# A hybrid layer on one core: two key projections and a gate block change places in the state space stage

## The chip, the cores and the metric

The kernel runs on one core of a Trainium2 chip. The metric is the device time of one execution in microseconds, the median of several; lower is better. All times of instructions come from one profiled execution.

The core has TensorE (PE: matmuls, and transposes made as matmuls), VectorE (DVE), ScalarE (ACT), GpSimd (POOL) and SyncE (SP), which issues the DMAs here. Each engine works through its own instructions in order and waits on semaphores for the others. Matmul results go to PSUM, in banks of 128 x 512 fp32.

## What is computed

One layer for 512 tokens of width 1024: a normed input is projected; a state space mixer (S5) and an attention with compressed, selected and windowed keys (NSA) work on parts of the projection; gates merge them; a feed-forward part with a convolution and a last gated part follow. The pieces that matter here:

```python
z = n1 @ w_in[i]
y_ssm = s5_mixer(z[..., OFF_SSM:OFF_Q], ...)
y_nsa = nsa_mixer(z[..., OFF_Q:OFF_KV], z[..., OFF_KV:OFF_NSA_GATE], ...)
merge = jax.nn.sigmoid(z[..., OFF_MERGE:].astype(jnp.float32))
mixed = merge[..., :D_MODEL] * (y_ssm @ w_br_ssm[i]) + merge[..., D_MODEL:] * (y_nsa @ w_br_nsa[i])

# s5_mixer: a linear recurrence over time, 32 groups of 64 complex states
_, states = lax.associative_scan(combine, (a_seq, bu), axis=1)
y = einsum(c_re, real(states)) - einsum(c_im, imag(states))
# nsa_mixer: keys of blocks of 32 tokens are made by a small network
kc = compress_blocks(k_cmp, pe_k, wk1, wk2)
vc = compress_blocks(v_cmp, pe_v, wv1, wv2)
```

All of it is in fp32. A product of two fp32 matrices is made of three matmuls of rounded parts: high x high, low x high, high x low.

## The kernel before

**Projections.** `proj` (L202 and on, with `mm3` at L81 to L84) multiplies one 128-column block of `w_in` with the normed input: 8 x 3 = 24 matmuls of 512 columns into a PSUM bank of the tag `acc`, of which there are two. The weights are brought by a DMA on SyncE's queue into one of three buffers `wr`; ScalarE copies their high part `wh` (L75), and GpSimd or VectorE subtracts it to get the low part `wl` (L54). There are two buffers each of `wh` and `wl`, so the weights of one projection can only be split when the projection two places before it has let go of them. In this stage GpSimd makes `wl`.

**The state space stage** works in four quarters. `ssm_quarter` is a generator in two halves. The first half prepares a quarter: products `z` (VectorE) and `x` (GpSimd) of the recurrence's coefficients, spread by ScalarE into `Z` and `CX`, transposed on TensorE (`wbps`, L798), copied by ScalarE (`WB`), and multiplied with the inputs (`wps`, L807). The second half makes its outputs: VectorE rotates (`f`, `wps`), runs four scans (L852) with small carries `c` between, and rotates back into the states `sr`; TensorE makes a small matrix `tps` (L832), which ScalarE copies as `tz`; then TensorE multiplies `sr` and `tz` into `yps` (L870, L872), VectorE adds a skip term (`un`) and ScalarE takes the gelu (`yT`).

**What else runs there**: `compress_in(i)`, a projection whose result ScalarE and VectorE copy, two copies each, into `FL`; `keys(br)`, a projection whose result goes to `KK`, the high part by ScalarE and the low part by VectorE, half by half (a half's subtraction by VectorE needs ScalarE's copy of that half); `compress(i)`, 32 small matmuls `hps` (L917), a transposing copy `hT`, a gelu `hid` on ScalarE and a last product `kps` (L932 or L942); and `gate_done(i)`, a projection with a tanh into `t1`. Behind the stage follow the softmaxes of `compressed`, with the gates 1 to 3 between them, a gated unit `glu`, and attention, whose matmuls are mixed with more gate projections.

**What sets the order.** The code is recorded by a scheduler, which orders each engine's instructions itself: mainly by the order in which the code hands them over, by when it expects their inputs, and by edges written with `issue_after`, which hold instructions back behind a named one. It also hands out the PSUM banks of a tag. A call that stands earlier in the code thus goes ahead of what follows it where both could go.

Of the kernel before, what the change touches and what calls it, by code (L numbers as in the profile page):

```python
# [44 lines left out]
def hybrid_kernel(ctx: ExitStack, tc: tile.TileContext, A, out):  # L45
# [7 lines left out]
    def tt(o, a, b, op, e=V):  # L53
        e.tensor_tensor(o, a, b, op=op)  # L54
# [19 lines left out]
    def copy(o, a):  # L74
        S.activation(o, a, AF.Copy)  # L75
# [27 lines left out]
    def slot(p, tag, shape, dt, name):  # L103
        return p.tile(shape, dt, tag=tag, name=name, bufs=1)
# [97 lines left out]
    def proj(c0, e=V, w=None):  # L202
        hi, lo = w or wload("w_in", INW, 0, c0, KD, P, e)
        ps = bank("acc", "pj")
        for k in range(KD):
            mm3(ps, hi[:, k], lo[:, k], n1h[:, k], n1l[:, k], k == 0, k == KD - 1)
        return ps
# [686 lines left out]
    def compress_in(i):  # L894
        ps = proj(OFF_KV + i * P, G)
        for g in range(2):
            for j in range(2):
                x = ps[64 * g:64 * g + 64, j:j + 1]
                (V.tensor_copy if g else copy)(
                    FL[64 * j:64 * j + 64, i, :, g, 0:NCMP - 1],  # L900
                    bass.AP(tensor=x.tensor, offset=x.offset, ap=[x.ap[0], [2, 16], [16, NCMP - 1]]))

    def keys(br):
        ps = proj(OFF_KV + 256 + 256 * br, G)
        for g in range(2):
            s0, o0 = 64 * g, 64 * (1 - g)
            copy(KK[s0:s0 + 64, br, g], ps[s0:s0 + 64])
            tt(KK[o0:o0 + 64, br, g], ps[s0:s0 + 64], KK[s0:s0 + 64, br, g], SUB)
# [44 lines left out]
    def t1(dt_):  # L953
        return t1s[dt_ // 4][:, dt_ % 4]

    def gate(dst, w):
        ps = bank("acc", "pj")
        for k in range(KD):
            mm3(ps, w[0][:, k], w[1][:, k], n1h[:, k], n1l[:, k], k == 0, k == KD - 1)
            yield  # L960
        S.activation(dst, ps, AF.Tanh, scale=0.5)

    def gate_weights(i, e=G):
        return wload("w_in", INW, 0, OFF_M + i * P, KD, P, e)

    def gate_done(i):
        for _ in gate(t1(i), gate_weights(i)):
            pass
# [3 lines left out]
    for q in range(4):  # L972
        if q < 3:
            next(quarters[q + 1])
        next(quarters[q])
        if q == 0:
            compress_in(0)
            compress_in(1)
        elif q == 1:
            compress(0)  # L980
            keys(0)
            t1s.append(slot(py, "t8", [P, 4, T], F32, "t1a"))
        elif q == 2:
            VC = compress(1)
            keys(1)
            gate_done(0)
    sM.close()
    sS.close()
    PTC = slot(pa, "ptc", [P, 2, 2, T], F32R, "PTC")

    def compressed(qt):
        qs_ = slice(qt * P, (qt + 1) * P)
        ps = bank("s", "cs")
        for i in range(4):
            PE.matmul(ps[:, P * i:P * i + P], QT[:, i, 0, qs_], KC[:, :, i // 2], start=True, stop=False)
            PE.matmul(ps[:, P * i:P * i + 64], QT[:, i, 1, qs_], KC[:, 0, i // 2], start=False, stop=True)
        sc = pw.tile([P, H, NCMP], F32, name="cmps", tag="mg")
        shc = [P, H, NCMP]
        sums = ps.rearrange("p (i x h n) -> p x i h n", i=4, x=2, h=2)
        sc4 = sc.rearrange("p (i h) n -> p i h n", i=4)  # L1000
        tt(sc4, sums[:, 0], maskc[:, qt, None, None, :].to_broadcast([P, 4, 2, NCMP]), ADD)
        tt(sc4, sc4, sums[:, 1], ADD)
        mx, su = small("cmx", H, 2), small("csu", H, 2)
        V.tensor_reduce(mx, sc, AX.X, ALU.max)
        tt(sc, sc, mx[:, :, None].to_broadcast(shc), SUB)
        with tc.issue_after(ys_at) if qt >= 2 else nullcontext():
            S.activation(sc, sc, AF.Exp, scale=HD ** -0.5)
        V.tensor_reduce(su, sc, AX.X, ADD)
        V.reciprocal(su, su)
        tt(su, su, gates[:, qt, 0:8], MUL)  # L1010
        if qt == 0:
            ts(su, su, rowok)
        tt(sc, sc, su[:, :, None].to_broadcast(shc), MUL)
        return sc

    def compressed_t(qt, sc):
        pc = bank("t", "pct")
        for g in range(2):
            PE.transpose(pc[:, g * P:(g + 1) * P], sc[:, 4 * g:4 * g + 4].rearrange("p h n -> p (h n)"), ident)
        qs_ = slice(qt * P, (qt + 1) * P)  # L1020
        split(PTC[:, 0, :, qs_], PTC[:, 1, :, qs_], pc[:, 0:256].rearrange("p (g t) -> p g t", g=2))
# [11 lines left out]

    scs = {}
    for dt_ in range(4):
        if dt_:
            gate_done(dt_)
        scs[dt_] = compressed(dt_)
        if dt_:
            compressed_t(dt_ - 1, scs[dt_ - 1])  # L1040
# [697 lines left out]
    with tc.manual_schedule(engines={mybir.EngineType.PE, mybir.EngineType.SP}):  # L1738
# [328 lines left out]
        keys = {"22": 0, "s1": 1, "s2": 2, "s3": 3, "s4": 0}  # L2067
# [192 lines left out]
```

## Time and profile before

| | us |
|---|---|
| median of 3 runs | 785.84 (785.81 to 785.86) |
| the profiled execution | 786.37 |
| its span, from the first to the last instruction | 784.6 |
| VectorE busy | 611.0 |
| ScalarE busy | 437.0 |
| GpSimd busy | 233.3 |

The span is a little shorter than the execution that it was taken from. Busy times add up what an engine did. A timeline row gives an instruction's start, its duration, the engine, the line, output and inputs, shapes and a count of merged instructions, and in square brackets how long the engine had been idle before it and who released it. Matmuls overlap, so the time that one really costs is the distance between two starts and not the duration in its row. A matmul of fp32 operands that are not split shows as two in the trace and as one in the order of the program.

### The profile page before, as it was taken

What the parts mean: (1) busy time and instruction counts of PE and PEld (TensorE: products, weight loads), DVE (VectorE), ACT (ScalarE), POOL (GpSimd) and SP (SyncE); (2) the same over time, 40 slices, a digit from 0 to 9 for tenths busy, and PEclk for the clock granted to TensorE, in tenths of its full rate; (3) what the DMA queues carried; (4) which work ended last, traced back from release to release, by engine and by line L of the source; (5) the groups of instructions that cost most, each with busy time, mean ns of one, the idle gap of its engine ahead of it and who ended that gap; (6) DMA issues with size and microseconds to landing.
All of it is one profiled execution on the core that took longest, in us unless ns stands there. A gap on an engine that the chain in (4) does not pass through costs nothing.

```text
span 784.6 us, 12279 instructions
## 1 busy us (share of the span) xinstructions
PE 767.0 (98%) x4362; PEld 646.7 (82%) x4362; DVE 611.0 (78%) x1192; ACT 437.0 (56%) x779; POOL 233.3 (30%) x263
## 2 busy tenths in 40 slices
PE   9999999999999999999999999999999999999993
PEld 7887778888888888888998888888888888888883
DVE  7987999776677739799757887988977586877586
ACT  6835645656676745444644554455444555645654
POOL 3577533126464625001032122221222110000125
PEclk9999999999999999999999999999999999999997
DMA  9954131423234327310266887778887366578752
GB/s 343 372 160 150 54 96 42 126 78 114 75 93 124 108 72 277 103 33 27 82 215 219 286 296 263 262 255 294 318 266 267 115 252 213 206 231 289 271 215 107
DMA packets 52077, 144.54 MB, mean 184 GB/s; under 512 B 6192, under 2 KB 8624, under 8 KB 52016
## 3 DMA queue, kind: packets, MB, share of 16 engines
q1 hardware_dynamic: 51440, 142.71, 53.1%
q10 hardware_dynamic: 576, 1.05, 0.4%
q8 instruction: 34, 0.56, 0.3%
q14 instruction: 27, 0.22, 0.1%
HBM read 112.28 MB, written 27.26 MB: 178 GB/s over the span
## 4 chain that ended last, share of the span: by engine, by line
PE 87%; DVE 6%; DMA 2%; issue 2%; ACT 1%; POOL 1%; SPq 0%; POOLq 0%; DVEq 0%; ACTq 0%
PE pj L82 6%; PE pj L83 6%; PE pj L84 6%; PE ua L1664 5%; PE ua L1665 5%; PE ub L1664 5%; PE ub L1670 5%; PE ua L1670 5%; PE ub L1665 5%; PE p L84 4%; PE p L82 4%; PE p L83 4%; PE sps L1089 2%; PE ptp L1109 2%; PE br L82 2%; PE br L84 2%
## 5 line engine op out<-in xcount | busy, mean ns | idle before, releaser
L54 POOL TENSOR_TENSOR wl<-wr,wh 128x1024 fp32r<-128x1024 f32 x45 | 114.4, 2543 | 315.0 <-ACT wh L75 185.7
L75 ACT ACTIVATE wh<-wr 128x1024 fp32r<-128x1024 f32 x96 | 100.7, 1050 | 59.8 <-issue 19.8
L82 PE MATMUL pj<-n1h,wh 128*128 128x512 f32 x224 | 90.9, 406 | 0.5 <-DVE QT L54 0.5
L83 PE MATMUL pj<-n1l,wh 128*128 128x512 f32 x224 | 87.9, 392 | 0.0
L84 PE MATMUL pj<-n1h,wl 128*128 128x512 f32 x224 | 87.8, 393 | 0.0
L54 DVE TENSOR_TENSOR wl<-wr,wh 128x1024 fp32r<-128x1024 f32 (+1 forms) x51 | 62.0, 1216 | 18.6 <-ACT wh L75 18.6
L1664 PE MATMUL ua<-n2h,wh 128*128 128x512 f32 x160 | 62.4, 390 | 0.0
L1665 PE MATMUL ua<-n2l,wh 128*128 128x512 f32 x160 | 62.3, 389 | 0.0
L1664 PE MATMUL ub<-n2h,wh 128*128 128x512 f32 x160 | 62.3, 389 | 0.0
L1665 PE MATMUL ub<-n2l,wh 128*128 128x512 f32 x160 | 62.2, 389 | 0.0
L63 DVE SCALAR_TENSOR_TENSOR cv<-ua,cols,cv 128x511 f32<-128x511 f32 (+1 forms) x44 | 32.9, 749 | 23.5 <-ACT cv L1511 22.7
L84 PEld LDWEIGHTS pj<-n1h,wl 128*128 128x128 f32 x224 | 42.1, 188 | 8.8
L82 PEld LDWEIGHTS pj<-n1h,wh 128*128 128x128 f32 x224 | 42.1, 188 | 8.3 <-DVE QT L54 0.9
L83 PEld LDWEIGHTS pj<-n1l,wh 128*128 128x128 f32 x224 | 42.2, 188 | 7.4 <-issue 0.2
L63 DVE SCALAR_TENSOR_TENSOR cv<-ub,cols,cv 128x511 f32<-128x511 f32 (+1 forms) x44 | 32.9, 748 | 15.8 <-ACT cv L1511 14.8
L60 POOL TENSOR_SCALAR pr<-pr,su,gates 128x512 f32<-128x512 f32 (+2 forms) x64 | 38.6, 619 | 16.6 <-DVE su L1101 16.3
L75 ACT ACTIVATE ph<-ptp 128x128 fp32r<-128x128 f32 (+1 forms) x64 | 27.8, 435 | 26.2 <-PE ptp L1109 26.0
L54 DVE TENSOR_TENSOR pl<-ptp,ph 128x128 fp32r<-128x128 f32 (+1 forms) x64 | 31.0, 486 | 14.3 <-ACT ph L75 13.3
L1670 PE MATMUL ub<-n2h,wl 128*128 128x512 f32 x160 | 39.5, 389 | 0.0
L1670 PE MATMUL ua<-n2h,wl 128*128 128x512 f32 x160 | 39.5, 389 | 0.0
L75 ACT ACTIVATE ffa<-cv 128x256 fp32r<-128x256 f32 x22 | 9.2, 418 | 53.0 <-DVE cv L54 46.5
L1100 ACT ACTIVATE pr<-pr,nb 128x512 f32<-128x512 f32 (+2 forms) x64 | 35.5, 558 | 3.0 <-DVE nb L1098 2.9
(522 smaller groups left out, 2091.7 us busy)
## 6 DMA issues: line engine op xcount, KB each, us to landing
wr<-in_w_up_dram SPq DMA_DIRECT2D x44, 512.0 KB, 4.4
wr<-in_w_in_dram SPq DMA_DIRECT2D x28, 512.0 KB, 3.8
b<-in_w_down_dram SPq DMA_DIRECT2D x22, 512.0 KB, 6.0
bs<-b SPq DMA_DIRECT2D x44, 256.0 KB, 5.5
ue<-bs SPq DMA_DIRECT2D x21, 512.0 KB, 4.8
wr<-in_w_down_dram SPq DMA_DIRECT2D x11, 512.0 KB, 5.3
gs<-gph SPq DMA_DIRECT2D x10, 512.0 KB, 6.1
gs<-gpl SPq DMA_DIRECT2D x10, 512.0 KB, 6.8
```

Of the source, the lines that this page charges most:

```text
L54: e.tensor_tensor(o, a, b, op=op)
L60: e.tensor_scalar(o, a, s1, s2, op0=op0, op1=op1)
L63: e.scalar_tensor_tensor(o, a, s, b, op0=op0, op1=op1)
L75: S.activation(o, a, AF.Copy)
L82: PE.matmul(ps, lh, rh, start=start, stop=False, skip_group_check=goes_on)
L83: PE.matmul(ps, lh, rl, start=False, stop=False, skip_group_check=goes_on)
L84: PE.matmul(ps, ll, rh, start=False, stop=stop, skip_group_check=goes_on)
L1089: PE.matmul(o, self.QQ[:, x, qt * P:(qt + 1) * P], KK[:, :, self.g, :w] if both else KK[:, self.br, self.g, :w], start=x == 0, stop=x == 1)
L1100: S.activation(pp, pp, AF.Exp, bias=nb, scale=-1.0, accum_out=su)
L1664: PE.matmul(ps, hi[:, k], n2h[:, k], start=k == 0, stop=False)
L1665: PE.matmul(ps, hi[:, k], n2l[:, k], start=False, stop=False)
L1670: PE.matmul(ps, lo[:, k], n2h[:, k], start=False, stop=k == KD - 1)
```

## The change

In the loop over the quarters `keys(0)` and `keys(1)` are called ahead of the outputs of quarters 0 and 1, not behind those of quarters 1 and 2. `gate_done(1)` is called behind the outputs of quarter 3, and no longer between the softmaxes of `compressed`.

```diff
     for q in range(4):
         if q < 3:
             next(quarters[q + 1])
+        if q < 2:
+            keys(q)
         next(quarters[q])
         if q == 0:
             compress_in(0)
             compress_in(1)
         elif q == 1:
             compress(0)
-            keys(0)
             t1s.append(slot(py, "t8", [P, 4, T], F32, "t1a"))
         elif q == 2:
             VC = compress(1)
-            keys(1)
             gate_done(0)
+        else:
+            gate_done(1)
     sM.close()
...
     for dt_ in range(4):
-        if dt_:
+        if dt_ > 1:
             gate_done(dt_)
```

The projections of the stage used to come in the order compress_in(0), compress_in(1), keys(0), keys(1), gates 0 to 3. Now it is keys(0), compress_in(0), compress_in(1), keys(1), gates 0 to 3. Since the scheduler decides, the order of the built programs shows what that moves.

TensorE around the first outputs of quarter 0, before (`hps` is the first part of compress(0), `sr` the states of quarter 0, `pj` a projection, here the end of compress_in(1)):

```order
L84 MATMUL pj<-n1h,wl 128x512
L917 MATMUL hps<-wk_1007,FL 64x128 x15
L870 MATMUL yps<-sr_991,CX_977 32x128 x4
L798 MATMUL wbps<-ident,Z_972 128x128 x4
L917 MATMUL hps<-wk_1007,FL 64x128
L870 MATMUL yps<-sr_990,CX_976 32x128 x4
L872 MATMUL yps<-Uc,tz 32x128 x4
```

The same place in the changed program (`pj` is now compress_in(1), of which 20 matmuls stand ahead of these rows):

```order
L83 MATMUL pj<-n1l,wh 128x512
L870 MATMUL yps<-sr_991,CX_977 32x128 x4
L84 MATMUL pj<-n1h,wl 128x512
L82 MATMUL pj<-n1h,wh 128x512
L83 MATMUL pj<-n1l,wh 128x512
L84 MATMUL pj<-n1h,wl 128x512
L798 MATMUL wbps<-ident,Z_972 128x128 x4
L870 MATMUL yps<-sr_990,CX_976 32x128 x4
L872 MATMUL yps<-Uc,tz 32x128 x4
```

The projection compress_in(1) has moved ahead of these outputs; compress(0)'s 32 matmuls have moved behind `tps` of quarter 1, between the first `yps` of that quarter and the ones that need `tz`.

VectorE ahead of quarter 0's scans (L852), before:

```order
L54 TENSOR_TENSOR wps<-wps,tab_915 128x512
L899 COPY FL<-pj 64x16x31 x2
L54 TENSOR_TENSOR f_1117<-wps,tab_914 128x512
L54 TENSOR_TENSOR wps<-wps,tab_915 128x512
L54 TENSOR_TENSOR wps<-f_1117,wps 128x512
L54 TENSOR_TENSOR wps<-f_1116,wps 128x512
L852 SCALAR_TENSOR_TENSOR wps<-dec,wps 128x256 x2
```

and now:

```order
L54 TENSOR_TENSOR wps<-wps,tab_915 128x512
L54 TENSOR_TENSOR KK<-pj,KK 64x512
L54 TENSOR_TENSOR f_1152<-wps,tab_914 128x512
L54 TENSOR_TENSOR wps<-wps,tab_915 128x512
L54 TENSOR_TENSOR wps<-f_1152,wps 128x512
L54 TENSOR_TENSOR wps<-f_1151,wps 128x512
L54 TENSOR_TENSOR KK<-pj,KK 64x512
L852 SCALAR_TENSOR_TENSOR wps<-dec,wps 128x256 x2
```

The FL copies of the first projection are replaced by the two subtractions of keys(0); one FL pair now stands ahead of the first scan of quarter 1, as a pair did before, and the other between its first and second scan.

GpSimd from a first `x` product of quarter 2 on, before (`wl` is a split of weights, `x` a product for quarter 2):

```order
L54 TENSOR_TENSOR x_1332<-PI,CT 128x320
L840 MEMSET dec 128x4
L54 TENSOR_TENSOR wl<-wr,wh 128x1024
L54 TENSOR_TENSOR x_1331<-PR,CT 128x320
L54 TENSOR_TENSOR x_1331<-x_1331,x_1332 128x320
```

and now:

```order
L54 TENSOR_TENSOR x_1367<-PI,CT 128x320
L840 MEMSET dec 128x4
L54 TENSOR_TENSOR wl<-wr,wh 128x1024 x2
L54 TENSOR_TENSOR x_1366<-PR,CT 128x320
L54 TENSOR_TENSOR x_1366<-x_1366,x_1367 128x320
```

Two splits now follow each other, those of keys(1) and gate(0), where before gate(0)'s came after the `x` products of that quarter.

## The prediction

> **What bounds the kernel now.** I read the busy table first, then windows over the state space stage, the list of what TensorE waited for, and the timelines of TensorE, VectorE, ScalarE and GpSimd there.
>
> ```profile
> span 784.6 us, 12279 instructions
> PE 767.0 (98%) x4362; PEld 646.7 (82%) x4362; DVE 611.0 (78%) x1192; ACT 437.0 (56%) x779; POOL 233.3 (30%) x263
> ...
> 93.00:115.00 22.00, 19.27 (x310) 15.82 (x313) 21.80 (x44) 12.48 (x27) 9.54 (x9) 1.00 0.21 63
> 115.00:161.00 46.00, 46.00 (x586) 39.77 (x576) 38.54 (x91) 25.44 (x44) 8.84 (x6) 1.00 0.32 92
> ```
>
> TensorE bounds the kernel. In a window row the columns behind the length are the busy time of TensorE, its weight loads, VectorE, ScalarE and GpSimd. From 93 to 115 us the bound changes hands: TensorE idles 2.73 us and VectorE is busy 21.80 of 22. From 115 to 161 us TensorE never idles. The idle time of the first stretch is three waits:
>
> ```profile
> 92.74 0.40 PE L84 MATMUL pj<-n1h,wl 128*128 128x512 f32 x1
> 93.07 1.96 PE L917 MATMUL hps<-wk,FL 128*64 128x128 f32 x30
> ...
> 97.52 0.43 PE L870 MATMUL yps<-sr,CX 128*32 128x128 f32 x8 [1.18 <-DVE sr L54]
> ...
> 111.81 0.43 PE L870 MATMUL yps<-sr,CX 128*32 128x128 f32 x8 [0.76 <-DVE sr L54]
> ...
> 114.63 0.43 PE L872 MATMUL yps<-Uc,tz 128*32 128x128 f32 x8 [0.79 <-ACT tz L75]
> ```
>
> They are the outputs of quarter 0 (1.18) and of quarter 1 (0.76, 0.79). The amounts of matmul work stay as they are, so all that the change can win is 1.18 + 0.76 + 0.79 = 2.73 us, and it keeps what is left after its own new waits are taken off. The profiled execution took 786.37 us around its span of 784.6 and lies 0.53 above the median of 785.84; I carry the difference over to the median. About 0.2% (1.57 us) is what a measurement of this kernel can tell from no change.
>
> **TensorE's own time to quarter 1's outputs.** Ahead of quarter 0's outputs TensorE now has a whole projection instead of the `hps` matmuls, which took 1.9 us. What each piece takes is read between its start and the next one's; the last two rows enclose a projection of 24 matmuls:
>
> ```profile
> 95.32 0.66 PE L798 MATMUL wbps<-ident,Z 128*128 128x128 f32 x4
> ...
> 100.06 1.16 PE L807 MATMUL wps<-Uc,WB 128*128 128x128 f32 x8
> 101.06 0.56 PE L922 MATMUL hps<-ident,hT 128*128 128x64 f32 x4
> ...
> 109.45 1.38 PE L832 MATMUL tps<-CX,Z 128*32 128x128 f32 x64
> 110.59 0.46 PE L870 MATMUL yps<-sr,CX 128*32 128x128 f32 x8
> ...
> 147.49 0.48 PE L82 MATMUL pj<-n1h,wh 128*128 128x512 f32 x1
> ...
> 153.05 0.22 PE L995 MATMUL cs<-KC,QT 128*128 128x128 f32 x1
> ```
>
> The projection is 5.56 us, 0.23 each with 0.3 for the first. From 92.97, where the next projection can start, to the last `sr` of quarter 1 TensorE has two projections (11.1), quarter 0's outputs (a first yps group of 0.36, and 2.54 from 97.52 to 100.06), two groups of wbps (0.59 at most each, 0.9 together), two of wps (1.0 each, 2.1 with a switch of kind), tps (1.14, or 1.25 with wps in its midst) and the first yps (0.35): 18.6 us, so without waits it arrives at 111.6. The wait of 1.18 goes: at 99.4 TensorE asks for an `sr` that VectorE has by 98.0 (96.79 + 0.67 before, + 0.5 below).
>
> **VectorE's chain to that `sr`.** This chain has no idle time, so every instruction put into it moves its end. Rows of before:
>
> ```profile
> 84.47 1.37 DVE L899 COPY FL<-pj 64x496 f32<-64x496 f32 x2
> 85.87 0.69 DVE L54 TENSOR_TENSOR f<-wps,tab 128x512 f32<-128x512 f32 x1
> ...
> 88.26 1.27 DVE L852 TENSOR_TENSOR_SCAN wps<-dec,wps 128x256 f32<-128x256 f32 x2
> ...
> 96.79 0.67 DVE L54 TENSOR_TENSOR sr<-f,wps 128x512 f32<-128x512 f32 x1
> ...
> 100.56 0.42 DVE L54 TENSOR_TENSOR z<-z,z 128x256 f32<-128x256 f32 x1
> 100.90 1.26 DVE L852 TENSOR_TENSOR_SCAN wps<-dec,wps 128x256 f32<-128x256 f32 x2
> ...
> 105.73 1.26 DVE L852 TENSOR_TENSOR_SCAN wps<-dec,wps 128x256 f32<-128x256 f32 x2
> ...
> 111.08 0.67 DVE L54 TENSOR_TENSOR sr<-f,wps 128x512 f32<-128x512 f32 x1
> 111.78 0.68 DVE L54 TENSOR_TENSOR KK<-pj,KK 64x512 fp32r<-64x512 f32 x1
> 112.50 0.69 DVE L54 TENSOR_TENSOR f<-wps,tab 128x512 f32<-128x512 f32 x1
> ```
>
> First, the pair of FL copies at 84.47 (1.40 with their gap) leaves and two KK subtractions come in its place, 0.72 each. The second one needs ScalarE's second KK copy, and that stands behind the filling of tps:
>
> ```profile
> 86.97 0.59 ACT L826 ACTIVATE tps<-ident 128x512 f32<-128x512 f32 x1
> ...
> 108.77 0.58 ACT L75 ACTIVATE KK<-pj 64x512 fp32r<-64x512 f32 x1
> ```
>
> It runs at 87.45 to 88.03, the subtraction at 88.06, and the scan queued behind it on VectorE at 88.78 instead of 88.26: **+0.52**.
>
> Second, one FL pair now stands between the two scans of quarter 1, behind the first and ahead of the second, while one z product moves behind the second scan: 1.40 in, 0.33 to 0.87 out of the stretch and 0.33 back behind it. I take **+0.96**.
>
> Third, a collision. A z product of VectorE reads two SBUF tiles. When GpSimd is at work, it does not end before GpSimd's instruction does:
>
> ```profile
> 76.37 2.42 POOL L54 TENSOR_TENSOR wl<-wr,wh 128x1024 fp32r<-128x1024 f32 x1 [0.58 <-ACT wh L75]
> ...
> 103.72 0.93 POOL L54 TENSOR_TENSOR x<-x,x 128x320 f32<-128x320 f32 x1
> ...
> 77.54 1.53 DVE L54 TENSOR_TENSOR z<-PZ,bb 128x256 f32<-128x256 f32 x1
> 103.99 0.94 DVE L54 TENSOR_TENSOR z<-z,z 128x256 f32<-128x256 f32 x1
> ```
>
> The z ops end at 79.07 and 104.93, GpSimd's at 78.79 and 104.65: 0.28 later both times, where a z op alone takes 0.42. The change gives GpSimd two weight splits in a row. ScalarE makes the next weights' high part as soon as the projection two places earlier lets go of the buffer; that projection now ends ahead of quarter 0's outputs (last L83 at 98.9) and not after them. High part 99.0 to 100.05 (1.06 in the row below), GpSimd's split from 100.13 to 102.5. VectorE's z sum, at 100.56 before, stands at 101.08 with the first term: right in it. It ends at 102.8 instead of 101.5, and with it wait the scans of quarter 1, queued behind it, and ScalarE's Z copy, from which TensorE has its next wbps: **+1.32**.
>
> [...]
>
> So quarter 1's `sr` ends at 111.75 + 0.52 + 0.96 + 1.32 = 114.55, and TensorE, due at 111.6, has waited **3.05** by then (part of it earlier, at wbps and the first `sr`, which hang on the same chain). For the third term the ends are 0 (GpSimd comes after the z sum) and 2.4 (one whole split); the row it is nearest to is the 1.53.
>
> **From there on.** The wait for tz (0.79) goes, since the 32 `hps` matmuls now lie ahead of it, 2.0 us, and ScalarE has tz by then. A new one comes. `kps` (L932) needs `hid` from ScalarE, where it now stands behind Z, dec and CX of the next quarter:
>
> ```profile
> 93.93 1.06 ACT L75 ACTIVATE wh<-wr 128x1024 fp32r<-128x1024 f32 x1
> ...
> 117.82 0.85 ACT L75 ACTIVATE Z<-z 64x256 f32<-64x256 f32 x2 [0.69 <-DVE z L54]
> 118.68 0.95 ACT L75 ACTIVATE CX<-x 64x320 f32<-64x320 f32 x2
> 120.22 0.42 ACT L75 ACTIVATE dec<-rho 128x256 f32<-128x256 f32 x1 [0.59 <-DVE wps L852]
> ...
> 121.15 0.17 ACT L75 ACTIVATE pe<-hps 128x1 f32<-128x1 f32 x1
> 121.35 0.31 ACT L930 ACTIVATE hid<-hps,pe 128x64 f32<-128x64 f32 x1
> ```
>
> TensorE, from 114.6: yps 0.35, hps 2.0, the rest of yps 2.33 (as at 114.63), hT 0.37, wbps 0.45, hps 1.9: at kps at 122.0. VectorE: the two products of quarter 2, KK, two sums, z, scan, KK, scan, z, some 0.6 each, the z sum done at 120.25. ScalarE then needs 0.85 + 0.42 + 0.95 + 0.17 + 0.31 and gaps, 2.8 in all: hid at 123.0. TensorE waits **1.0**, with gate(0) queued behind (between 0, if dec and CX slip ahead of z, and 1.6).
>
> Everything later has cover. Quarter 3's `sr` is ready near 140.5, TensorE asks near 143; the two softmaxes that now run together end near 157.5, their transposes are asked for near 159.5, behind one and a half gate blocks. One of those blocks is gate(1), moved into quarter 3; in before the same gates stood between the softmaxes, so there they no longer cover, but two remain. Two of the three table loads around them go too, on ScalarE, for which nobody waits there. On SyncE's queue a few loads change places with a neighbour (keys(1)'s weights go ahead of a block of cmp_wv1), and a load lands in 3.8 us, while a weight buffer is refilled two projections, 11 us, before its turn:
>
> ```profile
> wr<-in_w_in_dram SPq DMA_DIRECT2D x28, 512.0 KB, 3.8
> ```
>
> From early attention on, each engine has its old order, on a TensorE without idle time, so the shift arrives at the end whole.
>
> **Sum:** 3.05 + 1.0 - 2.73 = +1.3 us: 787.7 for an execution like the profiled one, 787.1 us for the median.
>
> **The rivals.**
> *The collision misses.* GpSimd's split begins behind the z sum, or blocks it little. The third term is 0 and part of the second goes: `sr` at 112.6, waits 1.05 + 1.0, 0.7 less than now: 785.1. For it: only about a microsecond separates the z sum from the split's start. Against it: both hang on fixed chains.
> *The cover holds altogether.* `sr` at 112.6 as above, and hid ahead of TensorE: 1.05 of waiting instead of 2.73, 784.1. For it: two places of waiting get 24 matmuls each or the hps put ahead. Against it: VectorE had 0.2 us free of 22.
> *More collisions, slower.* GpSimd's three x products (0.73 to 0.93) shift with CX by the same time and catch the z products behind quarter 1's first scan, 0.5 each on a chain that TensorE waits for: +1.5 on the forecast, 788.6. It decides from 0.3 us beyond the forecast, where the 0.2% ends. For it: such a z took 0.94 at 103.99. Against it: I have two of them already in the second term.
>
> **How the numbers follow.** Forecast 0.46, of which 0.10 falls beyond the bound, since it lies only 0.3 below it; the missed collision 0.18; the cover 0.12; more collisions 0.24. Within 0.2%: 0.36 + 0.18 = 0.54; slower: 0.10 + 0.24 = 0.34; faster: 0.12. The range runs from the missed collision's 785.1, less 0.2 for the work between the waits, to 788.6 and 0.4 for the hid wait's upper end: 784.9 to 789.0.
>
> **What would show it.** Right: TensorE idle before quarter 0's yps gone; 2 to 3 us of idle by quarter 1's yps, for `sr` (some of it before wbps); none before tz; about 1 us before kps; a z sum near 101 us of over 1.4, ending 0.28 behind a GpSimd split. Wrong: a z sum of 0.42 there; a wait of more than a microsecond after 125 us; or waits that add up to less than 1.2 us.

## The result and the profile after

The changed kernel takes 790.94 us, the median of 4 executions (789.01 to 791.26), against 785.85 us for the kernel before (785.81 to 785.90, 4 executions). It is **slower by 0.6%**: the ratio is 1.006, with a 95% interval of 1.0044 to 1.0076. The prediction was 787.1 us, at most 789.0. It had the sign, but the loss is 5.1 us and not 1.3, which by its own bound of 1.57 could not be told from no change. More executions of the same kernel, told below, gave 790.66 us and a ratio of 1.005 (1.0037 to 1.0063).

The profiled execution took 791.26 us. The head of its page and the list of what TensorE waited for between 90 and 165 us (engine, waiting instruction, releaser, total, times, longest):

```profile
span 789.5 us, 12278 instructions
PE 770.6 (98%) x4362; PEld 648.4 (82%) x4362; DVE 608.3 (77%) x1192; ACT 433.8 (55%) x777; POOL 233.8 (30%) x263
```

```profile
PE kps L932 <- ACT hid L930: 2.3, 1, 2.3
PE yps L870 <- DVE sr L54: 1.6, 2, 1.3
PE wbps L798 <- ACT Z L75: 0.5, 1, 0.5
```

Of the old three waits, those of quarter 0's outputs (1.18) and for `tz` (0.79) are gone. The new sum is 0.52 + 0.31 + 1.27 + 2.26 = 4.36 us, against 2.73 before: 1.63 more. But the gated unit `glu`, which follows the stage, starts at 165.74 instead of 160.47, 5.27 later; at the end 4.9 of it is left (span 789.5 for 784.6). (0.3 of it is there already before the stage, at quarter 1's first `wps`: 89.53 for 89.22.) So more than half of the loss is not waiting. The first rows of `glu`, before and after:

```profile
160.47 0.48 PE L82 MATMUL glu<-ysta,wh 128*128 128x512 f32 x1
...
165.74 0.48 PE L82 MATMUL glu<-ysta,wh 128*128 128x512 f32 x1
```

The timeline of TensorE after the change shows where the rest is:

```profile
99.86 0.43 PE L870 MATMUL yps<-sr,CX 128*32 128x128 f32 x8
...
104.08 0.66 PE L798 MATMUL wbps<-ident,Z 128*128 128x128 f32 x4 [0.52 <-ACT Z L75]
...
110.15 0.41 PE L832 MATMUL tps<-CX,Z 128*32 128x128 f32 x4
110.49 1.16 PE L807 MATMUL wps<-Uc,WB 128*128 128x128 f32 x8
111.57 1.32 PE L832 MATMUL tps<-CX,Z 128*32 128x64 f32 x60
113.21 0.43 PE L870 MATMUL yps<-sr,CX 128*32 128x128 f32 x8 [0.31 <-DVE sr L54]
114.91 0.43 PE L870 MATMUL yps<-sr,CX 128*32 128x128 f32 x8 [1.27 <-DVE sr L54]
...
117.16 0.43 PE L872 MATMUL yps<-Uc,tz 128*32 128x128 f32 x8
...
124.73 0.43 PE L932 MATMUL kps<-hid,W 128*128 128x64 f32 x2 [2.26 <-ACT hid L930]
...
125.46 0.78 PE L82 MATMUL pj<-n1h,wh 128*128 128x512 f32 x1
126.04 0.63 PE L83 MATMUL pj<-n1l,wh 128*128 128x512 f32 x1
126.47 1.06 PE L798 MATMUL wbps<-ident,Z 128*128 128x128 f32 x4
127.32 1.83 PE L807 MATMUL wps<-Uc,WB 128*128 128x128 f32 x8
128.89 0.49 PE L84 MATMUL pj<-n1h,wl 128*128 128x512 f32 x1
```

Look at the last five rows. `wbps` takes 0.85 from its start to the next one's and `wps` 1.57, where other such rows of this timeline take 0.4 to 0.5 and 0.9 to 1.2. The windows over that place say why; the granted clock is the third number from the end:

```profile
123.00:127.00 4.00, 2.27 (x9) 1.74 (x10) 4.00 (x7) 3.15 (x9) 1.70 (x3) 0.81 0.13 23
127.00:131.00 4.00, 4.00 (x20) 3.67 (x19) 1.85 (x5) 2.01 (x6) 0.00 (x0) 0.76 0.47 174
```

From 125.46 to 128.89, for 3.43 us, right behind the wait of 2.26, TensorE ran at half its clock (a window of just that stretch has 0.51). That costs half of 3.43: **1.7 us**. In the kernel before the same windows stand at 1.00:

```profile
123.00:127.00 4.00, 4.00 (x26) 3.56 (x25) 3.60 (x8) 3.48 (x6) 0.95 (x1) 1.00 0.27 66
127.00:131.00 4.00, 4.00 (x95) 3.46 (x94) 3.91 (x6) 0.93 (x2) 1.45 (x1) 1.00 0.38 123
```

What is left is TensorE's own time. From quarter 1's first `wps` near 89 us to the first `glu`, I took from the timeline of TensorE the distance from each row's start to the next one's, less the idle time in brackets, and added it up by kind of matmul (us; dec late is `dec_late`, dec+split late `wl_last_dec`, compress early `compress_early`, all kernels of the experiments below):

```
             before   after  dec late  dec+split late  compress early
wait           2.73    4.36      2.85            2.02            2.68
pj            34.80   35.22     34.91           34.85           35.22
yps           11.61   12.13     11.87           11.85           11.72
wps            5.84    6.78      5.92            5.76            5.84
hps            5.16    5.17      5.06            5.06            5.18
tps            4.90    5.43      5.40            5.33            5.06
cs + pct       3.58    3.81      3.78            3.81            3.67
wbps           1.87    2.33      1.92            1.85            1.81
kps            0.76    0.98      0.98            0.97            0.76
work          68.52   71.85     69.84           69.48           69.26
in all        71.25   76.21     72.69           71.50           71.94
```

The amount of matmuls is the same in every column. Of after's extra 3.33 us of work 1.7 is the clock; **1.6** is what is left, and it goes mostly with the order in which the matmuls stand. The three columns behind it, with the clock at 1.00 and the keys ahead of the outputs, have 0.7 to 1.3 more work than the kernel before. Of these, dec late and dec+split late keep TensorE's order of the changed kernel and have 1.3 and 1.0 more; dec+split late has two waits fewer than dec late, and a row that stands ahead of a wait is counted here at its full length. So 1.6 is an upper figure for the order, and about 1 us the part that is there whatever the waits do. An example is in the rows above: the `tps` of quarter 1, 64 matmuls on 32 columns, is cut by a `wps` on 128 columns behind its first matmuls. From 110.15 to 112.90 (113.21 less its wait) the two take 2.75, and 2.66 in dec+split late, where no wait follows. In the kernel before they stood apart, `wps` here and `tps` from 109.45 to 110.59:

```profile
108.36 1.16 PE L807 MATMUL wps<-Uc,WB 128*128 128x128 f32 x8
```

That is 1.09 and 1.14, 2.23 together: 0.4 to 0.5 less than cut into each other, with one change fewer between 32 and 128 columns within these rows. No run shows such a change by itself.

So 1.63 of waiting, 1.7 of clock and the 1.6 that is left make the 4.96 us by which this stretch grew.

### The profile page after: what moved, and what is told of

Read it like the earlier page. It is cut to its first block, busy times and chain, and to the rows that moved or that the text cites. A ratio compares the mean times of both kernels' runs of the same rounds, so it can differ in the third digit from the quotient of the medians.

```text
span 789.5 us, 12278 instructions
## 1 busy us (share of the span) xinstructions
PE 770.6 (98%) x4362; PEld 648.4 (82%) x4362; DVE 608.3 (77%) x1192; ACT 433.8 (55%) x777; POOL 233.8 (30%) x263
## 4 chain that ended last, share of the span: by engine, by line
PE 87%; DVE 6%; DMA 2%; ACT 1%; issue 1%; POOL 1%; SPq 0%; POOLq 0%; DVEq 0%; ACTq 0%
PE pj L82 6%; PE pj L83 6%; PE pj L84 6%; PE ua L1666 5%; PE ua L1667 5%; PE ub L1666 5%; PE ub L1667 5%; PE ua L1672 5%; PE ub L1672 5%; PE p L83 4%; PE p L82 4%; PE p L84 4%; PE sps L1091 2%; PE ptp L1111 2%; PE br L82 2%; PE br L83 2%
```

## The experiments

The theories that the experiments were to tell apart: **A**, what goes beyond the forecast is `hid`, held behind `dec` on ScalarE, and the lower clock that follows that wait; **B**, the collision of VectorE's z sum with GpSimd's split is the root; **C**, switching between kinds of matmul carries it, and the slow rows are such switches; **D**, the low clock follows any bunch of waits. Each median stands against the kernel before in the same session, which took 786.3 to 786.5 us there. Two more theories, **E** and **F**, stand in the expectations of the runs that they concern.

Why `hid` was late shows on ScalarE and VectorE after the change:

```profile
120.84 0.84 ACT L75 ACTIVATE Z<-z 64x256 f32<-64x256 f32 x2 [3.13 <-DVE z L54]
122.89 0.41 ACT L75 ACTIVATE dec<-rho 128x256 f32<-128x256 f32 x1 [1.21 <-DVE wps L852]
123.21 0.93 ACT L75 ACTIVATE CX<-x 64x320 f32<-64x320 f32 x2
...
124.37 0.31 ACT L930 ACTIVATE hid<-hps,pe 128x64 f32<-128x64 f32 x1
...
121.52 1.27 DVE L852 TENSOR_TENSOR_SCAN wps<-dec,wps 128x256 f32<-128x256 f32 x2
```

`dec` has one buffer. The one for quarter 3 can't be written before the last two scans of quarter 2 have read theirs (121.52 to 122.79). ScalarE stands still for 1.21 us in front of it, with CX, `pe` and `hid` queued behind.

### dec behind hid (dec_late)

```diff
-    spread_at, so_at, latest = [], [], last
+    spread_at, so_at, hid_at, latest = [], [], [], last
...
-        copy(dec, rho4[:, pq, None].to_broadcast([P, 4, HC]))
+        with tc.issue_after(hid_at[0]) if q == 3 else nullcontext(): copy(dec, rho4[:, pq, None].to_broadcast([P, 4, HC]))
...
-        S.activation(h1, hps[:, 0:64], AF.Gelu_apprx_tanh, bias=pe)
+        S.activation(h1, hps[:, 0:64], AF.Gelu_apprx_tanh, bias=pe); hid_at.append(latest(mybir.EngineType.Activation))
```

Expected:

> The changed kernel with one edge more: ScalarE's dec of quarter 3 is held behind hid, so hid no longer stands behind an instruction that waits for quarter 2's last scans. Theory A (hid behind dec, and TensorE's lower clock after that long wait): hid comes as soon as the second group of hps at 119.5 to 119.8 is done and ScalarE is past Z (ends 121.7) and CX (0.93), about 123.1 at the latest; kps waits 0.3 to 0.8 us instead of 2.26, the granted clock stays at 1.00 from 123 to 131, and the time falls by 1.5 to 2.0 for the wait and 1.4 to 2.0 for the clock, to 787.0 to 788.0. Theory B (the collision on VectorE carries the loss): kps waits less, but TensorE then waits for the next product of the same late chain; 790.3 to 791.0. Theory C (switching between kinds of matmul carries the loss; the slow rows at 125.5 to 128.9 are such switches): only the wait goes, 789.0 to 789.5.

Measured: 787.45 us (787.18 to 788.07), ratio 1.0015 (1.0006 to 1.0024). Rows of TensorE and ScalarE, then the windows:

```profile
122.93 0.43 PE L932 MATMUL kps<-hid,W 128*128 128x64 f32 x2 [0.75 <-ACT hid L930]
...
124.92 0.60 PE L798 MATMUL wbps<-ident,Z 128*128 128x128 f32 x4
125.36 1.06 PE L807 MATMUL wps<-Uc,WB 128*128 128x128 f32 x8
126.17 0.48 PE L84 MATMUL pj<-n1h,wl 128*128 128x512 f32 x1
...
122.56 0.31 ACT L930 ACTIVATE hid<-hps,pe 128x64 f32<-128x64 f32 x1
122.78 0.41 ACT L75 ACTIVATE dec<-rho 128x256 f32<-128x256 f32 x1
```

```profile
123.00:127.00 4.00, 4.00 (x25) 3.36 (x26) 3.71 (x7) 2.56 (x6) 1.07 (x3) 1.00 0.41 131
127.00:131.00 4.00, 4.00 (x29) 3.41 (x31) 2.03 (x5) 1.97 (x7) 0.00 (x0) 1.00 0.28 70
```

The wait is 0.75 instead of 2.26, the clock stays at 1.00, and four of the five us are back, by one edge on ScalarE. A's numbers hold. C, by which the slow rows were switches, falls for these rows: the same `wbps` and `wps` take 0.44 and 0.81 from start to start, where they took 0.85 and 1.57.

### GpSimd's split behind the x products (wl_late, and with dec: both_late)

```diff
-        for _ in gate(t1(i), gate_weights(i)):
-            pass
+        with tc.issue_after(x_at) if i == 0 else nullcontext(): w = gate_weights(i)
+        for _ in gate(t1(i), w): pass
...
-            next(quarters[q + 1])
+            next(quarters[q + 1]); x_at = last(mybir.EngineType.Pool) if q == 1 else None if q < 1 else x_at
```

`x_at` is GpSimd's last x product for quarter 2. Expected:

> The changed kernel with one edge more: GpSimd's split of gate(0)'s weights stands behind the three x products of quarter 2, as in the kernel before; TensorE, VectorE and ScalarE keep the order of the changed kernel. The z sum of quarter 2 (1.59 us) should then take 0.42. Theory A: the wait at wbps (0.52) goes, sr of quarter 1 is ready 1.2 earlier and its waits (0.31 + 1.27) shrink to 0.3 to 0.6; dec and hid come 1.2 earlier while TensorE comes 1.5 earlier, so the wait before kps stays at 2.3 to 2.6 and the low clock behind it too: 789.3 to 789.8. Theory B: all waits behind hang on the z sum, kps's too: 787.0 to 788.0, with a clock of 1.00. Theory C: as A.

> Both edges in the changed kernel: dec of quarter 3 behind hid, and GpSimd's split of gate(0)'s weights behind quarter 2's x products. Theory A: the gains add up, 1.2 to 1.6 from the z sum and 2.9 to 4.0 from hid and the clock: 785.5 to 786.8; what is left over the kernel before is only other order on TensorE. Theory B: as the z sum alone, 787.0 to 788.0. Theory C: the waits go but TensorE's own time stays 2 us longer: 787.5 to 788.2, with under 1 us of waits in the stage.

Measured: 789.88 us, ratio 1.0048 (1.0036 to 1.0061); with `dec` moved too 788.22, ratio 1.0023 (1.0014 to 1.0032), no better than `dec` alone. 789.88 is near A's figure, but not for A's reason, and with `dec` neither A's nor B's figure held, and C's only in its time: it had asked for waits under 1 us, and they came to 2.59. The collision had only moved. GpSimd, VectorE and TensorE with the split late:

```profile
104.86 2.58 POOL L54 TENSOR_TENSOR wl<-wr,wh 128x1024 fp32r<-128x1024 f32 x1
...
105.25 2.48 DVE L54 TENSOR_TENSOR z<-z,z 128x256 f32<-128x256 f32 x1
...
115.06 3.61 PE L917 MATMUL hps<-wk,FL 128*64 128x128 f32 x32
```

The first z sum takes its 0.42 now, but the second one, at 105.25, runs into the split, ends at 107.73, 0.29 behind GpSimd's 107.44, and the states `sr` come when they came. Here the clock fell earlier: the `hps` group took 3.6 instead of 1.9, behind waits of 0.81, 0.49 and 1.28 between 108.8 and 114.7. That speaks for D against the narrow reading of A, which had kept the wait before `kps` at 2.3 to 2.6; TensorE, slowed by then, waited 0.61 there. With `dec` moved too the profile has the same three waits (0.82, 0.49, 1.28) and a clock of 0.67 from 115 to 119 us behind them; 5 of its 11 executions had 0.992 and took 788.59 to 789.01, the other six 0.994 to 0.995 and 787.42 to 788.22.

### The split behind dec's memset (wl_last, and with dec: wl_last_dec)

```diff
-        for _ in gate(t1(i), gate_weights(i)):
-            pass
+        with tc.issue_after(last(mybir.EngineType.Pool)) if i == 0 else nullcontext(): w = gate_weights(i)
+        for _ in gate(t1(i), w): pass
```

GpSimd's last instruction is here the memset of `dec` for quarter 2. Expected:

> The changed kernel with GpSimd's split of gate(0)'s weights behind quarter 3's first x product and the memset of dec, from about 110.5: behind both z sums of quarter 2. TensorE, VectorE and ScalarE keep the order of the changed kernel. Both z sums (1.59 and 0.81 in the changed kernel) should take 0.4 to 0.8. Worked from the changed kernel's rows, sr of quarter 1 comes 1.2 to 1.5 earlier; the waits at wbps and at the first sr (0.52, 0.31) go, the second (1.27) falls to 0.5 to 1.0. Theory A (hid behind dec, and the clock that it lowers, are the loss beyond the forecast): 1.1 to 1.5 us faster than the changed kernel, so 3.5 to 4.0 above the kernel before, with a wait before kps of 2.0 to 2.5 and a low clock behind it still there. Theory B (the collision is the root of all of it): kps's wait goes as well, 0 to 1 above the kernel before. Theory D (the low clock follows any bunch of waits of 2 us, whatever they are): as A, but the low clock may come at either place.

> As the one before, and ScalarE's dec of quarter 3 behind hid. Theory A: 1.1 to 1.5 below the kernel with dec moved alone (which stood 1.1 above the kernel before), so 0 to 0.4 faster than the kernel before, waits of 1.0 to 1.8 in all in the stage, the granted clock at 1.00 through the stage. Theory B: no more than the split alone gave. Theory C (TensorE's own order costs some 1.3 whatever the waits do): waits 1.0 to 1.8, TensorE's work between the waits 69.8 us from quarter 1's first wps to glu as with dec moved alone, against 68.5 in the kernel before; that gives the same 0 to 0.4 faster as A and is told by this sum.

Measured: 789.39 us, ratio 1.0039 (1.0027 to 1.0052); with `dec` 786.32, ratio 0.9997 (0.9988 to 1.0006). The split alone:

```profile
100.88 0.43 DVE L54 TENSOR_TENSOR z<-z,z 128x256 f32<-128x256 f32 x1
...
105.26 0.81 DVE L54 TENSOR_TENSOR z<-z,z 128x256 f32<-128x256 f32 x1
...
113.06 0.43 PE L870 MATMUL yps<-sr,CX 128*32 128x128 f32 x8 [1.27 <-DVE sr L54]
...
122.89 0.43 PE L932 MATMUL kps<-hid,W 128*128 128x64 f32 x2 [2.25 <-ACT hid L930]
```

The collision is gone, and TensorE reaches this `yps` 1.85 earlier than in the changed kernel (1.2 of it if the 0.68 by which this execution runs ahead from before the stage is taken off). The waits at `wbps` and the first `sr` go, as A had it. But 1.27 and 2.25 stay: the two `sr` come 1.8 apart on VectorE with one `yps` group of 0.36 between them on TensorE, and `hid` moves up together with the rest. The time, 3.0 above the kernel before, is below A's range of 3.5 to 4.0 and far above B's. So B is wrong: the collision costs about 1 us (789.39 for the changed kernel's 790.66 in the same session, 786.32 for 787.45 with `dec` moved) and is not the root. With both edges the waits sum to 2.02, a little over A's range but less than before the change, the clock stays at 1.00, and yet the kernel is no faster than before: its 0.7 us less of waiting is taken by 0.96 more of own work. That part is what C says, though C doesn't say which switches carry it.

### kps behind compress(1) (kps_late)

```diff
-            compress(0)
+            kout = compress(0)
...
             VC = compress(1)
+            keys_out(*kout)
```

`keys_out` holds the product `kps` and its KC copies, taken out of `compress(0)`. Expected:

> The changed kernel with compress(0)'s last product kps and its KC copies handed over behind compress(1), so that they stand behind the first matmuls of gate(0); ScalarE keeps hid behind dec. Theory A: hid still comes at about 124.3, but TensorE has gate(0)'s matmuls and wbps to do by then; the wait of 2.26 shrinks to under 0.5 or moves, smaller, to wbps (its Z is there at 121.7), the clock stays at 1.00, and the time falls by 3 to 4 us from the changed kernel, to 1.0 to 2.0 above the kernel before. If hid itself (ScalarE's queue behind dec: WB, tz) were what holds everything, TensorE would wait as long for WB at wps, and the time would fall by less than 1 us.

Measured: 789.11 us, ratio 1.0039 (1.0025 to 1.0052): 2.7 above the kernel before, where A had 1.0 to 2.0. The wait did not shrink; it changed its name:

```profile
124.03 0.50 PE L82 MATMUL pj<-n1h,wh 128*128 128x512 f32 x1 [2.24 <-ACT hid L930]
```

gate(0)'s projection needs one of the two `acc` banks, and the one that comes free holds `hps`, which `hid` reads last. That is read from the code and the releaser: this projection has no other use for `hid`. `hid` thus held two things, the product and a PSUM bank. A's expectation missed this.

### More executions of the changed kernel (after_again)

> The changed kernel itself, more executions. Theory A or D (the clock is lowered for about 3.4 us by the waits in this stage, in most executions and not in all): the times fall into two groups, 789.0 to 789.6 with a mean granted clock of 0.995, and 790.7 to 791.6 with 0.992 to 0.993, 1.7 to 2.0 apart. If the clock has no part in it, the times spread without such groups, or do not go with the granted clock.

Measured: 790.66 us (789.53 to 791.36). With the first four, three executions took 789.01 to 789.70 at a mean granted clock of 0.994 to 0.995, and six 790.66 to 791.36 at 0.992 to 0.993. The means of the groups are 1.6 apart, about the 1.7 of one stretch at half clock. The stretch itself is seen only in the two profiled executions, both of the slower group; a mean of 0.993 alone doesn't prove it, since the kernel before has it too in executions that are not slower.

### The parts alone (gate_only, keys0_only, keys1_only, keys_only)

The first three are the kernel before with one of the three moves, the last the changed kernel with `gate_done(1)` back between the softmaxes. The edit of keys(0) alone; the others are made alike from the lines of the change:

```diff
+        if q == 0:
+            keys(0)
         next(quarters[q])
...
             compress(0)
-            keys(0)
```

Expected:

> The kernel before with gate_done(1) alone moved into quarter 3; both key projections stay where they were. Theory A: nothing of the three waits of the kernel before changes, no new wait, clock 1.00; what is left is the order of TensorE's matmuls (cs and pct cost 0.2 more in the changed kernel): within 0.5 of the kernel before. Theory E (the gate was the cover of the first softmaxes, and without it TensorE waits for pct or glu): a new wait of 1 us or more between 150 and 162 us and 1 to 2 us slower.

> The kernel before with keys(0) alone moved ahead of quarter 0's outputs. GpSimd's two splits stand in a row here too, so the z sum near 101 us should take 1.3 to 1.6; but hid stands ahead of the second Z and of dec on ScalarE. Theory A: no wait before kps over 0.5, clock 1.00; the wait of quarter 0's outputs (1.18) goes and quarter 1's get longer by 0.5 to 1.5: between 0.5 faster and 1.5 slower than the kernel before. Theory B (the collision is what costs): 3 to 5 us slower, as the whole change. Theory C (order on TensorE): 0.5 to 1.5 slower with unchanged sum of waits.

> The kernel before with keys(1) alone moved ahead of quarter 1's outputs. Two splits in a row on GpSimd again; hid stands ahead of dec on ScalarE. Theory A: no wait of 2 us before kps, clock 1.00, within 1.5 of the kernel before. Theory B: 3 to 5 us slower. Theory C: 0.5 to 1.5 slower with the sum of waits unchanged.

> Both key projections moved, gate_done(1) left between the softmaxes. Theory A: hid stands behind dec again, so the wait before kps is 2.0 to 2.5 with a lower clock behind it in most executions, and the time is that of the changed kernel less 0 to 0.5 for the gate: 4.0 to 5.0 above the kernel before, far above the sum of the two keys alone. Theory F (the parts add up and nothing is peculiar to the pair): the sum of the two single moves.

Measured: the gate alone 786.49, ratio 1.0002 (0.9994 to 1.0011); keys(0) alone 787.78, 1.0023 (1.0013 to 1.0033); keys(1) alone 790.37, 1.0057 (1.0044 to 1.0070); both keys 791.50, 1.0063 (1.0050 to 1.0077). The gate costs nothing that can be told from noise, so E falls, and both keys alone are the whole change (5.2, a little beyond A's range). keys(0) came out 1.5 slower, at the end of its range and well under B's, although its z sum took 1.58; keys(1) alone broke A's expectation. Its 4.1 is in B's range, but the z sum that B speaks of took 0.42 there (a z product behind the scans took 1.42). It has no `hid` behind `dec`, but other long waits:

```profile
PE wbps L798 <- DVE un L63: 2.2, 1, 2.2
PE wps L807 <- ACT WB L75: 1.7, 1, 1.7
PE hps L922 <- ACT hT L75: 0.7, 1, 0.7
```

So `hid` behind `dec` belongs to the two moves together, and each single move has a bill of its own. keys(0) alone had a wait of 2.79 for WB with the low clock behind it in its profile (0.92 from 93 to 115 us), and a mean clock of 0.991 to 0.993 in 5 of 9 executions. Theory F, that the parts add up, doesn't hold either: 1.5 and 4.1 make 5.6, near the pair's 5.2, but out of different waits.

### compress(0) ahead of the outputs (compress_early)

```diff
         if q < 2:
             keys(q)
+        if q == 1:
+            compress(0)
         next(quarters[q])
...
         elif q == 1:
-            compress(0)
             t1s.append(slot(py, "t8", [P, 4, T], F32, "t1a"))
```

with the split behind `dec`'s memset as above. Expected:

> The changed kernel with compress(0) handed over behind keys(1) and ahead of quarter 1's outputs, and with gate(0)'s split behind dec's memset. ScalarE then has hid ahead of the second Z and of dec, and quarter 1's first yps groups stand behind hps on TensorE and not ahead of it. Theory A (with what the earlier runs add: TensorE's waits, its clock and its order each to be counted): the wait of 1.27 at the second sr falls to 0.3 to 0.9 since TensorE arrives 1.9 later; kps waits 0.5 to 1.2 for hid; no wait of 2 us, clock 1.00; waits 1.0 to 2.1 in all, TensorE's own work 69.2 to 69.9 from quarter 1's first wps to glu: from 0.9 faster to 0.8 slower than the kernel before. If the keys ahead of the outputs cost for another reason than waits, clock and order, it stays 2 us or more slower.

Measured: 788.60 us (786.71 to 790.54), ratio 1.0040 (1.0026 to 1.0053). The second `sr` cost 0.60 and the work between the waits 69.26, as expected, but `kps` now comes right behind `hT` and waits 2.08 for `hid`, which stands on ScalarE behind a KK copy that waits 2.54 for VectorE. One execution kept a clock of 0.995 and took 786.71; the other four had 0.989 to 0.991 and took 788.39 to 790.54; these four were not profiled. As a better version it failed: with the clock up it only ties with the kernel before.

### Filler in place of the wait (filled_wait, filled_kps)

In the first, 18 matmuls without use, `PE.matmul(hps[:, 256:512], ...)`, behind `compress(1)`'s `hps` in the kernel with `kps` late; in the second 22 in the changed kernel right ahead of `kps`:

```diff
         if i == 0:
+            for _ in range(22):
+                PE.matmul(kps[:, 64:512], n1h[:, 0, 0:P], n1h[:, 0, 64:T], start=True, stop=True)
             PE.matmul(kps[:, 0:64], W2[:, 0:2].rearrange("p a d -> p (a d)"), h1, start=True, stop=True)
```

Expected:

> The kernel with kps handed over late, and 18 more matmuls of 256 columns on TensorE behind compress(1)'s hps, into columns of that bank that nothing reads: some 2.1 us of work of no use, in the place of the wait of 2.2 for hid. If it is the idling that lowers the clock: no wait over 1 us there, no stretch of half clock behind it, and every execution near the ones of the kernel without filler that kept a clock of 0.994 to 0.995: 1.8 to 2.9 above the kernel before, none of them 3.5 or more above. If the clock falls for another reason (the kind of work there, chance): executions at 0.992 to 0.993 and 3.5 to 4 above the kernel before come up as often as without filler, 2 in 5.

> The changed kernel, hid behind dec as in it, with 22 more matmuls of 448 columns on TensorE (4.2 us of no use, into columns of kps's bank that nothing reads) right ahead of kps: TensorE is busy until hid comes at about 124.4, and the second half of hps and a wbps, 2.3 us, follow behind kps and not ahead of it. Without a lowered clock that is 2.3 above the changed kernel's undisturbed executions, which stood 2.9 above the kernel before: 4.6 to 5.8 above the kernel before. If idling lowers the clock: no wait over 1 us from 119 us on, 1.00 in all stretches from 115 to 140, mean clock 0.994 to 0.995 and a spread of executions within 1 us. If the clock falls for another reason: 2 in 3 executions at 0.992 to 0.993 and 1.7 to 2 higher than the rest.

The first was inconclusive. The scheduler put a `wbps` between the fillers, TensorE waited 2.07 there instead, and the clock fell behind it again (0.93 from 123 to 127 us, 0.65 from 127 to 131); 791.72 us, 791.36 to 793.09. The second did what it should: 792.02 us (791.70 to 792.41), 5.5 above the kernel before, within its range. TensorE, and the windows:

```profile
119.54 4.70 PE L933 MATMUL kps<-n1h 128*128 128x448 f32 x22
124.33 0.43 PE L934 MATMUL kps<-hid,W 128*128 128x64 f32 x2
```

```profile
123.00:127.00 4.00, 3.91 (x35) 2.97 (x35) 3.60 (x6) 2.66 (x7) 1.65 (x3) 1.00 0.00 0
127.00:131.00 4.00, 4.00 (x101) 3.71 (x101) 2.48 (x6) 2.01 (x6) 0.00 (x0) 1.00 0.27 70
```

`kps` and ScalarE's `hid` come when they came (0.4 earlier, as all of this execution from 89 us on), and the idling ahead of `kps` is gone; the second half of `hps` and a `wbps`, which stood there, now follow behind `kps`. All five executions had a clock of 0.994 to 0.995 and lay within 0.7 us. Where the same wait was left idle, six executions of nine lost their clock, by their times. Together with dec late, where the wait was shortened another way and all 11 executions stayed within 0.9 us, this shows that it is the idling that lowered it here.

## Why the prediction was wrong, point by point

**What bounds the kernel**: right that TensorE does, and that its three old waits are all there is to win. But the step from there, "The amounts of matmul work stay as they are, so all that the change can win is 1.18 + 0.76 + 0.79", takes an equal amount for an equal time, and that failed: with 2.02 us of waiting left and the clock up, the kernel only came back to the old time.

**The waits that go**: right. Quarter 0's `yps` at 99.86 and `tz`'s at 117.16 have no idle time ahead of them.

**VectorE's chain**: right; its three terms came to 0.7, 0.9 and 1.2 for 0.52, 0.96 and 1.32. The row of the z sum, the split that blocked it, and the last `sr` of quarter 1:

```profile
101.56 1.59 DVE L54 TENSOR_TENSOR z<-z,z 128x256 f32<-128x256 f32 x1
...
114.18 0.67 DVE L54 TENSOR_TENSOR sr<-f,wps 128x512 f32<-128x512 f32 x1
...
100.48 2.39 POOL L54 TENSOR_TENSOR wl<-wr,wh 128x1024 fp32r<-128x1024 f32 x1 [2.59 <-ACT wh L75]
```

The z sum ends at 103.15, 0.28 behind GpSimd's 102.87, as forecast, and `sr` at 114.85 for 114.55, where 0.3 was there before the stage. The second z sum with the split late ended in the same way, 0.29 behind GpSimd's split.

**TensorE's own 18.6 us to that `sr`**: too short. From 93.28 to 114.91 are 21.63, less 2.10 of waiting 19.5. The wait by then was therefore 2.10 and not 3.05. The step read each piece between its start and the next one's, but in the old order; pieces that were cut apart took more. `tps` took 1.67 for 1.25, the two projections 11.35 for 11.1, and `wps` 2.24 for 2.1.

**`kps` and `hid`**: the wait was forecast and its place right, but 2.26 instead of 1.0. Here the step failed that says "between 0, if dec and CX slip ahead of z, and 1.6". It let `dec` run for the 0.42 of its row as soon as ScalarE was there. Its row was quoted with its own idle time, 0.59 behind a scan, and that is what it does: it waits for the readers of its one buffer. That cost 1.21 on ScalarE.

By chance the two errors nearly cancel: the waits were forecast at 4.05 in all and measured at 4.36. What broke the number is what the **sum** left out. It added waits and took TensorE's work between them as given; its range allows that work 0.2. That work grew by some 1.6, most of it through its order, and by 1.7 through the clock, which no term and no rival mentions, although a wait was forecast there. 1.3 + 0.3 (waits) + 1.6 + 1.7 + 0.3 (ahead of the stage) gives the 5.2 that `glu` moved.

**"Everything later has cover"**: right. No wait follows behind 125 us in the stage, and the gate block's move alone can't be told from nothing (786.49 for 786.27).

**The rivals**: none of them happened. "More collisions" had the right sign, but the four z ops behind quarter 1's first scan took 0.40, 0.43, 0.81 and 0.40, less than before (0.41, 0.59, 0.94 and 0.81).

**What would show it**: none of the signs of being wrong came, and all signs of being right did but the size of the wait before `kps`. They speak of waits and the z sum only, so they could not show what broke the number.

What stays open: which of the cuts on TensorE costs how much. The table shows kinds, not single places; a kernel that puts one cut back was not run.

## What to carry to other kernels

Price a new wait on TensorE not by its length alone: one of about 2 us could cost another 1.7 in clock, and the edge that removes it may sit on another engine. Before you take an instruction's finish from its row, walk the queue in front of it and ask of each entry which buffer it overwrites and who reads that last; a single buffer made a copy of 0.41 us into a barrier of 1.21 here. And when a change reorders TensorE, add up its work by kind before and after, less the waits: equal counts of matmuls did not make equal time here.

## What the runs showed of the hardware that I had not expected

**The clock fell after little idling.** One wait of 2.26 us halved TensorE's clock for 3.43 us; waits of 0.81, 0.49 and 1.28 within 6 us did so for 3.55 (the `hps` group above, 115.06 to 118.61; the clock of 0.57 in the window from 115 to 119 us makes it 3.4). It is not certain: a wait of 2.24 in the profile of kps late, one of 2.08 in that of compress early, and one of 2.15 with 0.66 close behind it in that of keys(1) alone left the clock at 1.00. The 27 executions of dec late, dec and split late and filler ahead of `kps`, whose longest wait in the profiles of this stage is 1.27, show no sign of it. So an idle time of 2.26, with work on both sides, was enough in the changed kernel; why the clock falls in one execution and not in another no run here explains.

**A PSUM bank was the real reason of a wait**: `kps` put out of the way left 2.24 of the 2.26 in front of the next projection, on the same releaser.
